# A hybrid attention and state-space step: chunk recurrence by pairs, fours and eights, the taps' own-input term in one operation, and a new placing of side steps

## The chip, the cores and the metric

The kernel runs on one core of one Trainium2 chip. The time is the device time of one execution in microseconds; the median of three runs before the change is 882.33 us. A core has five engines that this text names: TensorE (PE; its weight loads are PEld), VectorE (DVE), ScalarE (ACT), GpSimd (POOL) and SyncE (SP), which here issues all transfers (DMAs).

## What is computed

One layer of a streaming encoder, on 512 frames of one new stream and 16 further frames of each of 8 running streams (640 rows in all, 1024 channels), all in float32:

```python
h = rmsnorm(x, norm_g) @ w_in                     # 1024 -> 8 x 1024
q, k, v, ga, u, gs, gl = split(h)
o = diff_attn(rmsnorm(q), rmsnorm(k), v)          # 8 heads, two softmax maps, chunk-causal
ya = (rmsnorm(o) * silu(ga)) @ w_attn_proj
# diagonal complex state space, 64 groups x 64 states, 16 channels each
bu_t = B u_t ;  h_t = a * h_(t-1) + bu_t ;  y_t = Re(C h_t) + D u_t
ys = gelu(y);  ys = ys * sigmoid(ys @ w_glu + b_glu)
ys = (ys * silu(gs)) @ w_ssm_proj
x  = x + (sigmoid(g_a) * ya + sigmoid(g_s) * ys) @ w_out
# returned: x, the new k and v, the last state of each stream
```

The sample streams attend to a cache of 256 past keys and start from given states.

## The kernel before

**Products.** Every float32 product with a weight is three products of fp32r halves: an operand is split into a high part (ScalarE copies it, `whi`, `xh`) and the rest (VectorE subtracts, `wlo`, `xl`), and `mm3` (L306) adds hi x hi, hi x lo and lo x hi in PSUM. `gemm_a` (L401) computes 128 rows by 512 columns at a time for q, k, v and the last projection, `gemm_b` (L427) one block of 128 columns of the others for 2 x 320 rows. Weights come in pieces of 512 KB into `wraw`, two ahead, and are split by `pump` (L375). `ORDER` (L1581) is the list of these products with the columns of each; the main loop (L1490) goes through it.

**Side steps.** All else (norms, attention, the state space, the samples) is written as Python generators that yield a condition. The planner `Weave` (L38) keeps a model clock for each engine while the program is built. Between any two groups of three matmuls the main loop polls the generators, and whichever is due by the model puts its next piece into the program. TensorE runs in exactly this order; the other engines' instructions are ordered by a scheduler with a timeline model. `DELAY` (L1518, about 120 entries) adds microseconds to the due time of single steps, `GAPS` (L1553) a general gap in four stages. `lighter(bias)` (L63) picks VectorE or GpSimd for an elementwise piece: VectorE if its modelled queue ends before GpSimd's plus the bias. `W.hold()` moves the model's due time past the last transfer's landing. None of these is an instruction.

**The state space.** Time is cut into chunks of 8 frames: 64 chunks of the prompt, 2 for each sample stream. `ssm_setup` computes the powers of a, `ssm_f` and `ssm_in` the contribution of each chunk's inputs to the state at its end (`so`, stored as `s_d`). `ssm_tap` (L763) builds, in four parts q of 16 groups, `E` (powers times C, elementwise on VectorE or GpSimd, stored as `e_d`) and from it the taps: the direct effect of an input on the 8 outputs of its chunk. Its matmuls use plain float32 and a stationary operand of 32 columns, so that each writes 32 of the 128 PSUM partitions (index i) and 128 of 512 columns (index g). ScalarE copies the 128x512 result to `tp`; VectorE adds D u, the own-input term, to the first of the 8 taps, in four operations of 16 columns per q. `Es` has one buffer.

**The recurrence.** `states` (L1064) loads the 89 columns of chunk contributions as `R` (128 partitions x real/imaginary x 32 groups x 89): columns 0 to 15 are the samples' two chunks for 8 streams, 16 to 23 their start states, 24 to 88 the prompt. `cstep` takes a column range src to dst: two products with `a8` (a to the 8th, the step over one chunk), an addition, and an addition into R. It runs for the samples in 8 steps of 2 columns on GpSimd, and for the prompt 64 times, one column after the other, in pairs of steps that go to the engine that `lighter(ST_B)` names. Then `R` goes back to memory (`r_d`), for the output stage. The main loop has other waits on side steps: `kB` waits until the first half's 16 score steps are placed, `vB` until the first half's attention is stored; the samples' scores begin after the q's and `states`.

**Norms.** `norm_rows` (L815) and `subnorm` (L928) square on ScalarE, reduce on VectorE, and take the power -1/2 on GpSimd (`rs`, `osc`), then VectorE multiplies; TensorE then transposes the result (`kn`, `qn`, `o`).

Of the kernel before, what the change touches and what calls it, by code (L numbers as in the profile page):

```python
# [10 lines left out]
F32 = mybir.dt.float32  # L11
F32R = mybir.dt.float32r
AF = mybir.ActivationFunctionType
OP = mybir.AluOpType
# [8 lines left out]
RC = 89  # L23
# [170 lines left out]
CHAIN = object()  # L194
# [61 lines left out]
def trunk(nc, tc, a):  # L256
    es = ExitStack()
    enter = es.enter_context
    W = Weave(nc)
    PE, DV, AC, PL, SP = W.PE, W.DV, W.AC, W.PL, W.SP  # L260
# [17 lines left out]
    def mark(name):  # L278
        done.setdefault(name, []).append(W.t)
# [259 lines left out]
    a8 = pers.tile([128, 2, 2, 32], F32, name="a8")  # L539
# [223 lines left out]
    def ssm_tap(tpe):  # L763
        dT = tpe.tile([128, 4, 4], F32, name="dT")
        SP.dma_start(dT, a["dT"])
        dm = tpe.tile([128, 16], F32, name="dm")
        PL.tensor_tensor(dm, ident[:, 0:16], ident[:, 32:48], op=OP.add)
        PL.tensor_tensor(dm, dm, ident[:, 64:80], op=OP.add)
        PL.tensor_tensor(dm, dm, ident[:, 96:112], op=OP.add)
        PL.memset(bbs[:, 64], 0.0)  # L770


# [2 lines left out]
        tp = tpz[:, 7:]  # L775
        sh = [128, 4, 9, 16]
        for q in range(4):
            Es = tpe.tile([128, 4, 4, 144], F32, name="E", tag="E", bufs=1)
            for i in range(4):
# [5 lines left out]
                E = Es[:, i].rearrange("p g (j n) -> p g j n", n=16)  # L785
                Et = tpe.tile(sh, F32, name="Et", tag="Et", bufs=1)
                en = W.lighter()
# [3 lines left out]
                SP.dma_start(e_d[:, g4, :].rearrange("p g c -> p (g c)"), Es[:, i].rearrange("p g c -> p (g c)"))  # L791
                yield room("pv") if i == 3 else None
            pt = ps_pv()
            for i in range(4):
                for g in range(4):
                    gb = 16 * q + 4 * i + g
                    PE.matmul(pt[i * 32:i * 32 + 32, g * 128:g * 128 + 128],
                              bbs[:, gb:gb + 2, :].rearrange("p g n -> p (g n)"), Es[:, i, g, :128], start=True, stop=True)
            AC.activation(tp, pt.rearrange("p (g j n) -> p j g n", g=4, j=8), AF.Copy)
            for g in range(4):  # L800
                DV.scalar_tensor_tensor(tp[:, 0, g], dm, dT[:, q, g:g + 1], tp[:, 0, g], op0=OP.mult, op1=OP.add)
            SP.dma_start(tap_d[4 * q:4 * q + 4].rearrange("b n c -> (b n) c"), tpz.rearrange("p j g n -> p (j g n)"))
        mark("tap")

# [256 lines left out]

    def states(t3):  # L1064
        def cstep(E, dst, src, n):
            sh = [128, 2, 32, n]
            m1, m2 = (t3.tile(sh, F32, name="m12", tag=f"m{n}", bufs=2) for _ in range(2))
            E.tensor_tensor(m1, a8[:, 0, :, :, None].to_broadcast(sh), R[:, :, :, src:src + n], op=OP.mult)
            E.tensor_tensor(m2, a8[:, 1, :, :, None].to_broadcast(sh), R[:, ::-1, :, src:src + n], op=OP.mult)
            E.tensor_tensor(m1, m1, m2, op=OP.add)  # L1070
            E.tensor_tensor(R[:, :, :, dst:dst + n], R[:, :, :, dst:dst + n], m1, op=OP.add)

        R = t3.tile([128, 2, 32, RC], F32, name="R")
        SP.dma_start(R, s_d.rearrange("h p r g c -> (h p) r g c"))
        h0 = t3.tile([128, 2, 32, 8], F32, name="h0")
        SP.dma_start(h0, a["h0"])
        W.hold()
        yield
        AC.activation(R[:, :, :, 16:24], h0, AF.Copy)
        for d in (8, 0):  # L1080
            for i in range(0, 8, 2):
                cstep(PL, d + i, d + 8 + i, 2)
            yield CHAIN
        PL.tensor_copy(h0, R[:, :, :, 0:8])
        SP.dma_start(a["ss"], h0)
        for c in range(25, RC):
            if (c - 25) % ST_N == 0:
                yield CHAIN
                en = W.lighter(ST_B)
            cstep(en, c, c - 1, 1)  # L1090
        last = t3.tile([128, 2, 32], F32, name="last")
        PL.tensor_copy(last, R[:, :, :, RC - 1])
        SP.dma_start(a["sp"], last)
        SP.dma_start(r_d.rearrange("h p r g c -> (h p) r g c"), R)
        W.hold()
        mark("states")
# [393 lines left out]
    for n, opn, cols in ORDER:  # L1490
# [14 lines left out]
            gemm_a(op, evacs[n], *((lambda t: after("x", t + 1), FIRST) if n == "vA" else (None, GROUPS) if n == "o0" else ()))  # L1505
        else:
            gemm_b(op, evacs[n], cols, *((3, lambda i: after("og" if i else "og0")) if n == "ap" else ()))
        mark(n)
        if n == X_LAST:
            mark("xdone")  # L1510
        W.poll()
    pclose("ops", "yp")
# [3 lines left out]
COUNTERS = "hf", "t", "h4", "b", "b2", "first", "q", "x", "ct", "i", "gp", "m"  # L1516

DELAY = {  # L1518
# [30 lines left out]
}  # L1549
ACC = 0.6  # L1550
HALVES = slice(0, 64), slice(64, 128)
LATENCY = {"PE": 0.28, "AC": 0.2, "DV": 0.06, "PL": 0.3, "SP": 0.1}
GAPS = 1.3, 0.8, 0.4, 0.2  # L1553
SB = 3
WT = 2
ST_AT = 0
ST_N = 2
ST_B = 0.0
LANES = 3
SPB = 1  # L1560
# [3 lines left out]
TOB = 1  # L1564
KH = 4
VH = 6
X_LAST = "xs"
WRAW = 2
AHEAD = 5
FT = 2  # L1570
BIAS = 2.0
WARM = 10
GROUPS = ((0,), (1,), (2,), (3, 4))
FIRST = ((0,), (1,), (2,), (3,), (4,))
# [2 lines left out]
def cols(*names):  # L1577
    return [(n[0], n[1], range(*n[2:])) for n in names]


ORDER = [("vA", "x", None), ("u", "x", range(8)), ("kA", "x", None), ("ga", "x", range(8)), ("qA", "x", None),  # L1581
         ("gs", "x", range(0, 7)), ("kB", "x", None), ("qB", "x", None), ("vB", "x", None), ("gs", "x", range(7, 8)), ("xa", "x", range(0, 8)), ("xs", "x", range(0, 8)),
         ("ap", "og", range(8)), ("gl", "y", range(8)), ("sp", "y2", range(8)),
         ("o0", "m", None), ("o1", "m", None)]


OUTS = {"y": (TOK, 1024), "nk": (TOK, 1024), "nv": (TOK, 1024), "sp": (128, 2, 32), "ss": (128, 2, 32, 8)}

# [84 lines left out]
```

## Time and profile before

| | before |
|---|---|
| median of 3 runs | 882.33 us (880.16 to 882.72) |
| the profiled execution | 887.47 us, span 885.7 us |
| TensorE busy | 847.1 us, 5692 matmuls |
| VectorE busy | 558.9 us |
| ScalarE busy | 373.0 us |
| GpSimd busy | 253.0 us |
| mean granted TensorE clock | 0.987 of full speed |
| moved by DMA | 167.4 MB, 189 GB/s |

The span goes from the first to the last instruction; 1.8 us of the profiled execution lie around it. Busy times of different engines overlap. Matmuls are pipelined and one record's duration is longer than the distance to the next, so the idle time of TensorE is read from the gaps and the waits, not from single durations. Two full levels of the clock occur, 1.2 and 2.4 GHz; a share between is a mean over a stretch.

### The profile page before, as it was taken

Reading aid. Unit: us, or ns where it says so; the run is one execution under the profiler, and the core shown is the slowest. Engines: PE = TensorE matmul, PEld = TensorE weight load, DVE = VectorE, ACT = ScalarE, POOL = GpSimd, SP = SyncE. Lnnn points to the kernel's source line nnn. Section 1 sums busy time; section 2 is a strip of 40 time slices with the busy share of each in tenths; the row PEclk is TensorE's granted clock in tenths of the full one; section 3 lists DMA queues with packets and bytes.
Section 4 is the critical chain, followed back from the end, with each engine's and each line's share of the span. In section 5 each row is a group of like instructions: output and inputs, shape, how many; then the busy total and the mean of one; then the engine's idle time right before and its main releaser. Section 6 shows DMA issues by size and latency. Waiting matters only on the chain.

```text
span 885.7 us, 15567 instructions
## 1 busy us (share of the span) xinstructions
PE 847.1 (96%) x5692; PEld 776.9 (88%) x5692; DVE 558.9 (63%) x1267; ACT 373.0 (42%) x784; POOL 253.0 (29%) x426
## 2 busy tenths in 40 slices
PE   8999899889899989989999999999999999999998
PEld 6898889789789888767899887789999999999886
DVE  6688449886857788575667764224577755555321
ACT  6432227444236455233555544433565643422110
POOL 3734435323022996879810120000000000000000
PEclk8999899999899999999999999999999999999999
DMA  7365747564818531352585499958989763355231
GB/s 301 97 196 165 224 149 231 163 222 161 263 53 276 161 114 52 102 164 65 170 312 182 155 294 370 353 183 245 290 261 299 226 237 117 105 150 181 95 120 60
DMA packets 96445, 167.42 MB, mean 189 GB/s; under 512 B 16752, under 2 KB 54256, under 8 KB 96112
## 3 DMA queue, kind: packets, MB, share of 16 engines
q1 hardware_dynamic: 96368, 166.42, 59.1%
q8 instruction: 45, 0.74, 0.3%
q14 instruction: 32, 0.26, 0.1%
HBM read 118.45 MB, written 43.75 MB: 183 GB/s over the span
## 4 chain that ended last, share of the span: by engine, by line
PE 62%; POOL 12%; DMA 10%; DVE 10%; issue 3%; ACT 2%; SPq 1%; POOLq 0%; DVEq 0%; ACTq 0%
PE ps_mm L243 50%; POOL m L243 6%; PE ps_s L243 6%; DMA wraw<-in_wb_dram 4%; PE ps_pv L243 3%; PE ps_tp L243 3%; POOL R L243 3%; DVE wlo L243 2%; POOL rs L243 1%; ACT whi L243 1%; DMA svt<-in_cv_dram 1%; DMA H<-r_d 1%; DMA Ef<-e_d 1%; DMA u_d<-ue 1%; DVE kTl L243 1%
## 5 line engine op out<-in xcount | busy, mean ns | idle before, releaser
L243 PE MATMUL ps_mm<-xh,whi 128*128 128x320 f32 x640 | 205.5, 321 | 5.5 <-DVE ue L243 5.5
L243 PE MATMUL ps_mm<-xh,wlo 128*128 128x320 f32 x640 | 199.4, 312 | 0.0
L243 PE MATMUL ps_mm<-xl,whi 128*128 128x320 f32 x640 | 199.3, 311 | 0.0
L243 DVE TENSOR_TENSOR wlo<-wraw,whi 128x1024 fp32r<-128x1024 f32 x96 | 119.8, 1249 | 77.7 <-ACT whi L243 77.1
L243 ACT ACTIVATE whi<-wraw 128x1024 fp32r<-128x1024 f32 x96 | 101.6, 1059 | 109.7 <-PE ps_mm L243 79.6
L243 PEld LDWEIGHTS ps_mm<-xh,whi 128*128 128x128 f32 x640 | 121.9, 190 | 10.8 <-DVE ue L243 6.0
L243 PEld LDWEIGHTS ps_mm<-xl,whi 128*128 128x128 f32 x640 | 121.9, 190 | 0.8
L243 PEld LDWEIGHTS ps_mm<-xh,wlo 128*128 128x128 f32 x640 | 121.6, 190 | 0.0
L243 PE MATMUL ps_mm<-whi,xh 128*128 128x512 f32 x240 | 99.0, 412 | 0.9 <-ACT xh L243 0.9
L243 PE MATMUL ps_mm<-wlo,xh 128*128 128x512 f32 x240 | 95.6, 398 | 0.2 <-DVE wlo L243 0.2
L243 PE MATMUL ps_mm<-whi,xl 128*128 128x512 f32 x240 | 95.6, 398 | 0.0
L243 POOL TENSOR_TENSOR m<-a,R 128x64 f32<-128x64 f32 (+1 forms) x132 | 52.1, 418 | 15.4 <-DMA R<-s_d 8.2
L243 PEld LDWEIGHTS ps_mm<-whi,xl 128*128 128x128 f32 x240 | 46.1, 192 | 10.6 <-DVE xl L243 0.6
L243 PEld LDWEIGHTS ps_mm<-wlo,xh 128*128 128x128 f32 x240 | 46.3, 193 | 9.5 <-DVE wlo L243 1.4
L243 PEld LDWEIGHTS ps_mm<-whi,xh 128*128 128x128 f32 x240 | 46.3, 193 | 9.4 <-ACT xh L243 1.2
L243 POOL TENSOR_TENSOR rs<-ss,mhalf 128x8 f32<-128x8 f32 x20 | 32.9, 1645 | 40.8 <-DVE ss L243 40.6
L243 PE MATMUL ps_mm<-ogh,whi 128*128 128x320 f32 x128 | 41.0, 320 | 0.0
L243 PE MATMUL ps_mm<-yl,whi 128*128 128x320 f32 x128 | 39.6, 309 | 0.0
L243 PE MATMUL ps_mm<-yh,wlo 128*128 128x320 f32 x128 | 39.6, 309 | 0.0
L243 PE MATMUL ps_mm<-y2h,whi 128*128 128x320 f32 x128 | 39.6, 309 | 0.0
L243 PE MATMUL ps_mm<-y2h,wlo 128*128 128x320 f32 x128 | 39.6, 309 | 0.0
L243 PE MATMUL ps_mm<-y2l,whi 128*128 128x320 f32 x128 | 39.6, 309 | 0.0
(291 smaller groups left out, 1887.4 us busy)
## 6 DMA issues: line engine op xcount, KB each, us to landing
wraw<-in_wb_dram SPq DMA_DIRECT2D x64, 512.0 KB, 4.5
wraw<-in_wa_dram SPq DMA_DIRECT2D x32, 512.0 KB, 4.1
u<-u_d SPq DMA_DIRECT2D x16, 640.0 KB, 5.4
skt<-in_ckt_dram SPq DMA_DIRECT2D x16, 512.0 KB, 5.4
svt<-in_cv_dram SPq DMA_DIRECT2D x16, 512.0 KB, 8.0
u_d<-ue SPq DMA_DIRECT2D x16, 320.0 KB, 5.1
gate_xa<-gate SPq DMA_DIRECT2D x16, 320.0 KB, 4.1
e_d<-E SPq DMA_DIRECT2D x16, 288.0 KB, 3.4
```

The lines of the kernel that those rows point to most:

```text
L243: r = fn(out, *args, **kw)
```

## The change

Four things change.

1. `ssm_tap`: the loops over i and g of the tap matmuls change places, so that i runs inside. `dd`, the diagonal times D for all four q, is computed once by one VectorE product of 256 columns. Per q one VectorE addition of 64 columns reads the first tap from PSUM, adds `dd` and writes `tp`; ScalarE copies only the other seven taps. The planner holds for the transfer of `dT`.
2. `states`: `a16`, `a32`, `a64` are squared from `a8` by 18 small VectorE operations. The samples take one step of 8 columns for each of the two chunks. The prompt's chunks are combined in pairs (32, four pieces of 8), fours (16, two pieces), eights (8, one), then seven single steps over eights, then down again (7, 15 and 31 columns). Each piece is a `cstep` of up to 8 columns with a stride, on the engine that `lighter` names. The products' tile `m` has one tag with two buffers, which `h0` and the new `h1` share.
3. `DELAY` has new entries, `GAPS[2]` goes from 0.4 to 0.0 and `BIAS` from 2.0 to 1.36.
4. `ORDER`: the last column of `gs` comes after four columns of `xa`, and the columns of `xa` and `xs` are interleaved. `mark` and the end of the x operand's use follow the new list.

```diff
     def ssm_tap(tpe):
         dT = tpe.tile([128, 4, 4], F32, name="dT")
         SP.dma_start(dT, a["dT"])
+        W.hold()
...
+        dd = tpe.tile([128, 4, 4, 16], F32, name="dd")
+        sh = [128, 4, 4, 16]
+        DV.tensor_tensor(dd, dm[:, None, None, :].to_broadcast(sh), dT[:, :, :, None].to_broadcast(sh), op=OP.mult)
...
-            for i in range(4):
-                for g in range(4):
+            for g in range(4):
+                for i in range(4):
                     gb = 16 * q + 4 * i + g
                     PE.matmul(pt[i * 32:i * 32 + 32, g * 128:g * 128 + 128],
                               bbs[:, gb:gb + 2, :].rearrange("p g n -> p (g n)"), Es[:, i, g, :128], start=True, stop=True)
-            AC.activation(tp, pt.rearrange("p (g j n) -> p j g n", g=4, j=8), AF.Copy)
-            for g in range(4):
-                DV.scalar_tensor_tensor(tp[:, 0, g], dm, dT[:, q, g:g + 1], tp[:, 0, g], op0=OP.mult, op1=OP.add)
+            pj = pt.rearrange("p (g j n) -> p j g n", g=4, j=8)
+            DV.tensor_tensor(tp[:, 0], dd[:, q], pj[:, 0], op=OP.add)
+            AC.activation(tp[:, 1:], pj[:, 1:], AF.Copy)
...
     def states(t3):
-        def cstep(E, dst, src, n):
+        def cstep(E, A, dst, src, n, step=1):
             sh = [128, 2, 32, n]
-            m1, m2 = (t3.tile(sh, F32, name="m12", tag=f"m{n}", bufs=2) for _ in range(2))
...
+            cols = [slice(x, x + step * (n - 1) + 1, step) for x in (dst, src)]
+            m1, m2 = (t3.tile([128, 2, 32, ST_W], F32, name="m", tag="m", bufs=2)[:, :, :, :n] for _ in range(2))
+            E.tensor_tensor(m1, A[:, 0, :, :, None].to_broadcast(sh), R[:, :, :, cols[1]], op=OP.mult)
+            E.tensor_tensor(m2, A[:, 1, :, :, None].to_broadcast(sh), R[:, ::-1, :, cols[1]], op=OP.mult)
             E.tensor_tensor(m1, m1, m2, op=OP.add)
-            E.tensor_tensor(R[:, :, :, dst:dst + n], R[:, :, :, dst:dst + n], m1, op=OP.add)
+            E.tensor_tensor(R[:, :, :, cols[0]], R[:, :, :, cols[0]], m1, op=OP.add)
...
+        A = [a8] + [t3.tile([128, 2, 2, 32], F32, name=f"a{x}") for x in (16, 32, 64)]
...
         for d in (8, 0):
-            for i in range(0, 8, 2):
-                cstep(PL, d + i, d + 8 + i, 2)
-            yield CHAIN
-        PL.tensor_copy(h0, R[:, :, :, 0:8])
-        SP.dma_start(a["ss"], h0)
-        for c in range(25, RC):
-            if (c - 25) % ST_N == 0:
+            for i in range(0, 8, ST_W):
+                cstep(PL, a8, d + i, d + 8 + i, ST_W)
                 yield CHAIN
-                en = W.lighter(ST_B)
-            cstep(en, c, c - 1, 1)
+        h1 = t3.tile([128, 2, 32, 8], F32, name="h1", tag="m", bufs=2)
+        PL.tensor_copy(h1, R[:, :, :, 0:8])
+        SP.dma_start(a["ss"], h1)
+        up = [(A[x], 24 + (2 << x), 24 + (1 << x), 32 >> x, 2 << x) for x in range(3)]
+        row = [(A[3], 32 + 8 * k, 24 + 8 * k, 1, 1) for k in range(1, 8)]
+        down = [(A[x], 24 + (3 << x), 24 + (2 << x), (32 >> x) - 1, 2 << x) for x in (2, 1, 0)]
+        for Ax, dst, src, n, step in up + row + down:
+            for k in range(0, n, ST_W):
+                yield CHAIN
+                cstep(W.lighter(ST_B), Ax, dst + k * step, src + k * step, min(ST_W, n - k), step)
...
-GAPS = 1.3, 0.8, 0.4, 0.2
+GAPS = 1.3, 0.8, 0.0, 0.2
...
-BIAS = 2.0
+BIAS = 1.36
...
-         ("gs", "x", range(0, 7)), ("kB", "x", None), ("qB", "x", None), ("vB", "x", None), ("gs", "x", range(7, 8)), ("xa", "x", range(0, 8)), ("xs", "x", range(0, 8)),
-         ("ap", "og", range(8)), ("gl", "y", range(8)), ("sp", "y2", range(8)),
+         ("gs", "x", range(0, 7)), ("kB", "x", None), ("qB", "x", None), ("vB", "x", None), ("xa", "x", range(0, 4)),
+         ("gs", "x", range(7, 8)), ("xa", "x", range(4, 5)), ("xs", "x", range(0, 3)), ("xa", "x", range(5, 8)),
+         ("xs", "x", range(3, 8)), ("ap", "og", range(0, 8)), ("gl", "y", range(0, 8)), ("sp", "y2", range(0, 8)),
```

## Rows read from the trace of the kernel before

**Rows 1.** The page, busy times: us, share of the span, instructions.
```profile
PE 847.1 (96%) x5692; PEld 776.9 (88%) x5692; DVE 558.9 (63%) x1267; ACT 373.0 (42%) x784; POOL 253.0 (29%) x426
```
**Rows 2.** Sums by stretch: length, busy us (instructions) of each engine, granted clock, DMA.
```profile
140.00:240.00 100.00, 89.60 (x666) 86.65 (x665) 83.48 (x166) 45.34 (x107) 28.52 (x26) 0.95 0.66 209
220.00:240.00 20.00, 15.83 (x114) 14.90 (x113) 16.62 (x36) 7.50 (x20) 0.16 (x1) 0.86 0.77 253
300.00:440.00 140.00, 127.50 (x702) 108.86 (x701) 100.43 (x247) 60.58 (x131) 118.53 (x248) 1.00 0.37 108
712.00:880.00 168.00, 168.00 (x1024) 158.95 (x1023) 79.20 (x135) 45.97 (x73) 0.00 (x0) 1.00 0.42 136
```
**Rows 3.** TensorE's waits, whole span: releaser, us in total, times, longest.
```profile
PE ps_s L243 <- DVE tap L243: 4.2, 1, 4.2
PE ps_s L243 <- DVE so L243: 4.0, 3, 2.1
PE ps_tp L243 <- DVE kn L243: 2.8, 2, 2.2
```
**Rows 4.** Timeline of TensorE: start, us, operation, records; a tap group, one of scores.
```profile
229.12 2.46 PE L243 MATMUL ps_pv<-E,bbs 128*32 128x128 f32 x32
...
496.23 1.12 PE L243 MATMUL ps_s<-skt,qbd 128*32 128x272 f32 x16
```
**Rows 5.** Timeline after the first tap group, all engines; idle before and releaser in brackets.
```profile
163.54 3.10 DVE L243 SCALAR_TENSOR_TENSOR tap<-dm,dT,tap 128x16 f32<-128x16 f32 x3 [1.00 <-ACT tap L243]
...
165.21 1.40 POOL L243 TENSOR_TENSOR E<-E,Et 128x576 f32<-128x576 f32 x1
...
166.56 0.24 DVE L243 SCALAR_TENSOR_TENSOR so<-ps_s,sgn,so 128x32 f32<-128x32 f32 x1
...
166.95 0.31 PE L243 MATMUL ps_s<-u,Wh 128*128 128x160 f32 x1 [2.14 <-DVE so L243]
```
**Rows 6.** Timeline after the third tap group, VectorE and TensorE.
```profile
234.24 0.76 DVE L243 TENSOR_TENSOR E<-P,cc 128x576 f32<-128x576 f32 x1 [1.35 <-DMA wraw<-in_wb_dram]
...
235.75 0.47 PE L243 MATMUL ps_s<-u,Wh 128*128 128x160 f32 x1 [4.17 <-DVE tap L243]
```
**Rows 7.** Groups of VectorE by form: busy us, mean ns, idle before and releaser.
```profile
L243 DVE TENSOR_TENSOR o<-o,ps_pv 128x128 f32<-128x128 f32 x32 | 9.0, 281 | 1.5 <-ACT o L243 1.5
...
L243 DVE SCALAR_TENSOR_TENSOR tap<-dm,dT,tap 128x16 f32<-128x16 f32 x16 | 6.3, 447 | 1.0 <-ACT tap L243 1.0
```
**Rows 8.** Single tiles (`tap`, `F`, `P`): ns least/median/most, first and last start, forms.
```profile
L243 DVE SCALAR_TENSOR_TENSOR tap<-dm,dT,tap x16: 225/230/1430, 163.5 to 268.9; 128x16 f32<-128x16 f32 x16
...
L243 DVE TENSOR_TENSOR F<-F,Ft x9: 678/687/1646, 84.0 to 199.5; 128x512 f32<-128x512 f32 x9
...
L243 POOL TENSOR_TENSOR F<-F,Ft x7: 1265/1297/2157, 130.6 to 211.4; 128x512 f32<-128x512 f32 x7
...
L243 POOL TENSOR_TENSOR Ft<-P,bbi x7: 1100/1112/1544, 84.8 to 200.3; 128x512 f32<-128x512 f32 x7
```
**Rows 9.** Sum over the recurrence, tile `m` alone: length, DVE busy, POOL busy, clock, DMA.
```profile
284.00:441.00 157.00, 5.86 (x24) 109.47 (x264) 1.00 0.41 120
```
**Rows 10.** Timeline at the start of the recurrence, GpSimd and ScalarE.
```profile
284.57 0.67 POOL L243 TENSOR_TENSOR m<-a,R 128x64 f32<-128x64 f32 x2 [8.19 <-DMA R<-s_d]
...
287.57 0.67 ACT L243 ACTIVATE R<-h 128x512 f32<-128x512 f32 x1
```
**Rows 11.** Timeline of a key's norm within the recurrence, three engines.
```profile
394.86 1.64 POOL L243 TENSOR_TENSOR rs<-ss,mhalf 128x8 f32<-128x8 f32 x1
...
396.53 0.69 DVE L243 TENSOR_TENSOR kn<-ps_mm,rs 128x512 f32<-128x512 f32 x1 [1.84 <-POOL rs L243]
...
398.65 0.52 PE L243 MATMUL ps_tp<-ident,kn 128*128 128x128 f32 x3 [2.15 <-DVE kn L243]
```
**Rows 12.** Groups of GpSimd by form from 300 to 440: the powers of the norms.
```profile
L243 POOL TENSOR_TENSOR rs<-ss,mhalf 128x8 f32<-128x8 f32 x10 | 16.4, 1642 | 0.0
L243 POOL TENSOR_TENSOR osc<-oss,mhalf 128x4 f32<-128x4 f32 x4 | 4.9, 1235 | 0.0
```

More of the change, by code (lines that the diff above doesn't have):

```diff
@@ L1064, in states @@
     def states(t3):
-        def cstep(E, dst, src, n):
+        def cstep(E, A, dst, src, n, step=1):
             sh = [128, 2, 32, n]
-            m1, m2 = (t3.tile(sh, F32, name="m12", tag=f"m{n}", bufs=2) for _ in range(2))
-            E.tensor_tensor(m1, a8[:, 0, :, :, None].to_broadcast(sh), R[:, :, :, src:src + n], op=OP.mult)
-            E.tensor_tensor(m2, a8[:, 1, :, :, None].to_broadcast(sh), R[:, ::-1, :, src:src + n], op=OP.mult)
+            cols = [slice(x, x + step * (n - 1) + 1, step) for x in (dst, src)]
+            m1, m2 = (t3.tile([128, 2, 32, ST_W], F32, name="m", tag="m", bufs=2)[:, :, :, :n] for _ in range(2))
+            E.tensor_tensor(m1, A[:, 0, :, :, None].to_broadcast(sh), R[:, :, :, cols[1]], op=OP.mult)
+            E.tensor_tensor(m2, A[:, 1, :, :, None].to_broadcast(sh), R[:, ::-1, :, cols[1]], op=OP.mult)
             E.tensor_tensor(m1, m1, m2, op=OP.add)
-            E.tensor_tensor(R[:, :, :, dst:dst + n], R[:, :, :, dst:dst + n], m1, op=OP.add)
+            E.tensor_tensor(R[:, :, :, cols[0]], R[:, :, :, cols[0]], m1, op=OP.add)
         R = t3.tile([128, 2, 32, RC], F32, name="R")
         SP.dma_start(R, s_d.rearrange("h p r g c -> (h p) r g c"))
-        h0 = t3.tile([128, 2, 32, 8], F32, name="h0")
+        h0 = t3.tile([128, 2, 32, 8], F32, name="h0", tag="m", bufs=2)
         SP.dma_start(h0, a["h0"])
+        A = [a8] + [t3.tile([128, 2, 2, 32], F32, name=f"a{x}") for x in (16, 32, 64)]
+        sq = t3.tile([128, 32], F32, name="sq")
+        for x, y in zip(A, A[1:]):
+            re, im = x[:, 0, 0], x[:, 1, 1]
+            DV.tensor_tensor(sq, im, im, op=OP.mult)
+            DV.tensor_tensor(y[:, 0, 0], re, re, op=OP.mult)
+            DV.tensor_tensor(y[:, 0, 0], y[:, 0, 0], sq, op=OP.subtract)
+            DV.tensor_scalar(y[:, 0, 1], y[:, 0, 0], 1.0, None, op0=OP.mult)
+            DV.scalar_tensor_tensor(y[:, 1, 0], re, -2.0, im, op0=OP.mult, op1=OP.mult)
+            DV.scalar_tensor_tensor(y[:, 1, 1], re, 2.0, im, op0=OP.mult, op1=OP.mult)
+            yield CHAIN
         W.hold()
@@ L1080, in states @@
         for d in (8, 0):
-            for i in range(0, 8, 2):
-                cstep(PL, d + i, d + 8 + i, 2)
-            yield CHAIN
-        PL.tensor_copy(h0, R[:, :, :, 0:8])
-        SP.dma_start(a["ss"], h0)
-        for c in range(25, RC):
-            if (c - 25) % ST_N == 0:
-                yield CHAIN
-                en = W.lighter(ST_B)
-            cstep(en, c, c - 1, 1)
+            for i in range(0, 8, ST_W):
+                cstep(PL, a8, d + i, d + 8 + i, ST_W)
+                yield CHAIN
+        h1 = t3.tile([128, 2, 32, 8], F32, name="h1", tag="m", bufs=2)
[6 more added lines that the diff above has]
+            for k in range(0, n, ST_W):
+                yield CHAIN
+                cstep(W.lighter(ST_B), Ax, dst + k * step, src + k * step, min(ST_W, n - k), step)
         last = t3.tile([128, 2, 32], F32, name="last")
@@ L1507, in trunk @@
             gemm_b(op, evacs[n], cols, *((3, lambda i: after("og" if i else "og0")) if n == "ap" else ()))
-        mark(n)
-        if n == X_LAST:
+        if n in ("u", "ap"):
+            mark(n)
+        if (n, cols) == X_LAST:
             mark("xdone")
@@ L1556 @@
 ST_AT = 0
-ST_N = 2
+ST_W = 8
 ST_B = 0.0
@@ L1566 @@
 VH = 6
-X_LAST = "xs"
 WRAW = 2
@@ L1578, in cols @@
     return [(n[0], n[1], range(*n[2:])) for n in names]
-ORDER = [("vA", "x", None), ("u", "x", range(8)), ("kA", "x", None), ("ga", "x", range(8)), ("qA", "x", None),
-         ("gs", "x", range(0, 7)), ("kB", "x", None), ("qB", "x", None), ("vB", "x", None), ("gs", "x", range(7, 8)), ("xa", "x", range(0, 8)), ("xs", "x", range(0, 8)),
-         ("ap", "og", range(8)), ("gl", "y", range(8)), ("sp", "y2", range(8)),
+ORDER = [("vA", "x", None), ("u", "x", range(0, 8)), ("kA", "x", None), ("ga", "x", range(0, 8)), ("qA", "x", None),
+         ("gs", "x", range(0, 7)), ("kB", "x", None), ("qB", "x", None), ("vB", "x", None), ("xa", "x", range(0, 4)),
+         ("gs", "x", range(7, 8)), ("xa", "x", range(4, 5)), ("xs", "x", range(0, 3)), ("xa", "x", range(5, 8)),
+         ("xs", "x", range(3, 8)), ("ap", "og", range(0, 8)), ("gl", "y", range(0, 8)), ("sp", "y2", range(0, 8)),
          ("o0", "m", None), ("o1", "m", None)]
+X_LAST = [(n, cols) for n, operand, cols in ORDER if operand == "x"][-1]
 OUTS = {"y": (TOK, 1024), "nk": (TOK, 1024), "nv": (TOK, 1024), "sp": (128, 2, 32), "ss": (128, 2, 32, 8)}
```

59 rows, old and new, of the table DELAY are left out of this document.

## The prediction, made before the change was built

> **What bounds the kernel now.** I began with the page's busy times: TensorE is busy 847.1 us of a span of 885.7 [rows 1]. So the time is TensorE's work plus its idle time (38.6 us) plus what a lowered clock costs. The change leaves the matrix products as they are, so I looked for places where TensorE stands still or works badly, and asked which of them the change touches. The sums by stage show where that is: 10.4 us of idle time in 140 to 240 and 12.5 us in 300 to 440, while from 712 on TensorE never stops [rows 2]. An edit can pay in the first two stretches only. Third, TensorE's waits by releaser: VectorE's `tap` operations once for 4.2 us, its `so` evacuations three times for 4.0 us, its `kn` 2.8 us [rows 3]. They are single waits, not a steady shortage. In 300 to 440 GpSimd is the busiest engine after TensorE, 118.5 of 140 us [rows 2], nearly all of it the recurrence of `states`.
>
> **Part 1, the taps' matmuls.** This is the one edit that shortens TensorE's own work. Today the 16 products of one q are issued with i outside: four in a row go to the same 32 output partitions. Such a group shows as 32 records (each product is two) that take 2.46 us, and there are four groups [rows 4]. The new order lets i run inside, so neighbours go to four different strips of 32 partitions. The sample scores have that pattern already: 16 records of 272 columns, strips in turn, take 1.12 us [rows 4]. That is 16 x 272 = 4352 columns; a tap group has 32 x 128 = 4096, so I estimate 1.12 x 4096 / 4352 = 1.05 us, and allow 1.1. A group saves 1.36 us. Bounds: 0 (no overlap) and 1.41. The group near 229 is followed at once by a wait that VectorE ends [rows 4, 6], so there the gain only lengthens the wait; I count three: **-4.1 us**.
>
> **Part 2, the taps' own-input term.** Today ScalarE copies the whole 128x512 result out, and only then VectorE runs four small operations per q. 16 of them cost 6.3 us, 447 ns on average [rows 7], though 225 is the least [rows 8]. In the first group VectorE sat idle 1.00 us for the copy, then three took 3.10 us, and `so`, which TensorE needed, came at 166.56; TensorE had waited 2.14 us [rows 5]. After, one addition reads PSUM directly and is no longer behind ScalarE's copy. It has 64 columns; the nearest rows are the 128-column addition from PSUM at 281 ns and the small operation at 225 [rows 7, 8], so 0.28 us. At the first group that frees VectorE about 1.0 + 3.1 - 0.3 = 3.8 us earlier, more than the 2.14 us: **-2.1 us** (bounds 0 and -2.1). The same queue holds ScalarE's `so` copies behind a slightly shorter tap copy, which costs nothing.
>
> The 4.17 us wait at 235.75 is another matter. The profile names `tap`, but VectorE had before that stood 1.35 us at an `E` whose release was a transfer, then worked through `E` and the taps [rows 6]. With the operations in the same order the taps leave only 0.45 us there: **-0.45**, bounds 0 and -7.0. The far end is the whole wait plus the clock: the stretch 220 to 240 was granted 0.86 [rows 2], that is part of it at 1.2 instead of 2.4 GHz after that idle time, and 0.14 x 20 = 2.8 us of work is lost by it.
>
> New is `dd`, one product of 256 columns on VectorE before 90 us, between 0.28 (128 columns) and 0.69 us (512) [rows 7, 8], once. It also waits for the `dT` transfer, and behind it on VectorE's queue stand the first `E`, which need their own later transfer (`cc`) in any case. Cost 0, at most 0.7 if VectorE is the last to finish there. Holding the planner's clock until `dT` has landed adds no instruction.
>
> **Part 3, the recurrence.** It now runs 64 chunk steps one after the other, four operations each, 64 columns wide, and 8 sample steps of 128 columns: together 109.5 us of GpSimd and 5.9 of VectorE, from 284 to 441 [rows 9]. After: seven steps up (4 + 2 + 1), seven in a row, seven down (1 + 2 + 4), and two for the samples. 16 of the 23 are up to 8 chunks wide: 512 columns. No row shows that form of this step; the nearest are the 512-column operations for `F`: a product at 1.11 and the addition at 1.30 on GpSimd, 0.69 on VectorE [rows 8]. A wide step is then 2 x 1.11 + 2 x 1.30 = 4.8 us on GpSimd, or 2.8 on VectorE. A narrow one stays at 109.5 us over 66 steps, 1.7 us with the wider ones counted in, so at most that. All on GpSimd: 16 x 4.8 + 7 x 1.7 = 89 us, 20 less than today. Before, 24 of 288 instructions went to VectorE [rows 9]; the rule that chooses is the same, so I leave one step in ten there. Strided columns could make the wide form dearer; the old narrow form reads with a stride too. Bounds for the stage: 60 us (half on VectorE) and 110.
>
> What does it bring TensorE? Nothing waits for `states` but the samples, and TensorE has other columns to compute then; an earlier end alone is worth **0**. Two waits are added. `m`, `h0` and `h1` now share two buffers. The first wide step waits for ScalarE's copy of `h0`, done at 288.2, where today the chunk steps start at 284.6 [rows 10]: 3.6 us of GpSimd's time. Later a step waits until `h1` is stored. Queued behind on GpSimd are the powers of the norms; nobody else. The 18 small operations for the squared coefficients (near 0.23 us each by [rows 8], some 4 us) fall on VectorE while `R` is in flight: 0, at most +1.
>
> **Part 4, delays and order.** The table of delays, `GAPS`, `BIAS` and the order of the `gs`, `xa` and `xs` columns change where side steps fall among matmuls; columns cost the same anywhere, and the weights' transfers keep their number. No row prices this. It can take away stalls or make them: all idle time of both stretches, 22.9 us, is the one bound, and half as much more the other. For the middle I let idle time shrink as the load on the feeding engine does: VectorE in 140 to 240 loses about 16 x 0.447 - 4 x 0.28 = 6 of 83.5 us, 7% of 10.4 us; GpSimd in 300 to 440 loses some 18 of 118.5, 15% of 12.5 us: **-2.6 us**.
>
> **Sum.** -4.1 - 2.1 - 0.45 - 2.6 = -9.3 us. The profiled execution took 887.5 us (span 885.7 and 1.8 around it), so it would become 878.2. The median of the runs is 882.3, 5.1 lower; I carry the gain over in microseconds: **873.0 us**, 1.1% faster.
>
> **Rivals.** (a) *Slower: wide steps in the way of the norms.* GpSimd also computes the powers for `kn`, `qn` and `o`. At 394.86 such a power came between two operations of a chunk step; VectorE's `kn` waited 1.84 us for it and TensorE 2.15 us for `kn` [rows 11]. A step once queued will hold GpSimd 4.8 us where two chunk steps held it about 3.4. Also VectorE and GpSimd hinder each other: a `tap` operation beside GpSimd's `E` took up to 1.43 us against 0.23 and ended with it [rows 5, 8]. With operations of 1.1 to 1.3 us VectorE may wait up to 1.2 us where an operation of the present step lasts 109.5 / 264 = 0.41 [rows 9]. Price: 14 powers in the stretch [rows 12], each later by (4.8 - 3.4) / 2 = 0.7, and two VectorE operations behind each by 0.4 more: 14 x 1.5 = 21 us if all reaches TensorE. With the 6.7 us of parts 1 and 2 that is 897; with two thirds of it, 890. It decides for slower once more than 9.3 of the 21 us arrive. Against it: 12.5 us of idle time is all that the stretch shows today with GpSimd at 85%, and that share falls.
>
> The Trainium skill, page SBUF — State Buffer, section "SBUF: two separate sides", speaks against this change: it says that a VectorE operation with two SBUF inputs and a GpSimd operation take a shared pair of ports exclusively, for the whole instruction, and the other blocks fully. The 1.43 us row agrees with it; by this rule the case just priced would be the outcome, about 890.
>
> (b) *Much faster.* The wait at 235 with its clock goes, the fourth tap group counts too, and half the idle time of 300 to 440 goes: 4.1 + 1.4 + 2.1 + 7.0 + 6.3 = 21 us, 861.
>
> (c) *Nothing to measure.* The tap groups don't overlap, or TensorE runs sooner into the same evacuations; only some 2 us stay: 880 to 881.
>
> **Chances.** Forecast 0.57 (866 to 879.7), (b) 0.15, (c) 0.14, (a) 0.14. About 0.3% (2.6 us) is what a measurement of this kernel can tell from no change. Faster 0.72, same 0.14, slower 0.14. The range 862 to 886 leaves out the lower half of (b) and the larger part of (a).
>
> **What would show it.** Right: tap groups near 1.1 us; four `tap` additions of 64 columns near 0.3 us; no TensorE wait on `tap`; operations on `m` near 90 us on GpSimd in far fewer instructions, ended before 430. Wrong: groups still over 2 us; a TensorE wait on `kn` above today's 2.8 us; VectorE's two-input operations over 1 us beside GpSimd; new stalls outside both stretches.

## The result: 1.2% slower

The median of the kernel after is 892.41 us (891.24 to 893.47, four runs), that of the kernel before beside it 881.25 us; the ratio is 1.0120, 95% interval 1.0095 to 1.0146. The forecast was 873.0 us. The rows after that answer to [rows 1 and 2], the page's busy times and the sums by stretch (length, then busy us and instructions of TensorE, its weight loads, VectorE, ScalarE and GpSimd, granted clock, DMA share, GB/s):

```profile
PE 847.8 (95%) x5692; PEld 775.6 (87%) x5692; DVE 583.4 (66%) x1259; ACT 372.9 (42%) x784; POOL 249.5 (28%) x245
...
140.00:240.00 100.00, 92.49 (x685) 87.69 (x684) 86.22 (x160) 44.44 (x107) 35.39 (x31) 0.93 0.71 221
300.00:440.00 140.00, 123.97 (x664) 107.09 (x663) 114.07 (x215) 57.16 (x120) 107.66 (x92) 0.97 0.45 140
712.00:880.00 168.00, 166.40 (x1033) 157.57 (x1032) 80.27 (x137) 47.26 (x76) 0.00 (x0) 1.00 0.41 134
```

In 300 to 440 TensorE gets through 664 instructions instead of 702. GpSimd is less busy there than before (107.7 us against 118.5), as forecast; VectorE has fewer instructions (215 against 247) and is busy 13.6 us longer. That contradiction is the trail: VectorE's operations have become longer. The waits of TensorE, as [rows 3]:

```profile
PE ps_pv L243 <- DVE o L243: 7.6, 4, 4.3
PE ps_s L243 <- DVE so L243: 6.5, 5, 4.1
```

The wait on `o` for these products was, in the kernel before:

```profile
PE ps_pv L243 <- DVE o L243: 0.6, 2, 0.3
```

The wait on `tap` is gone. In its place stands one of 4.1 us on `so` at 223, and the one on `o` has grown from 0.6 to 7.6 us; it lies in the stage of the recurrence. The tap groups, as [rows 4], the additions to the first tap, and the recurrence's tile `m` on GpSimd (ns least, median, most; first and last start; forms; then idle time of its engine):

```profile
159.05 1.08 PE L243 MATMUL ps_pv<-E,bbs 128*32 128x128 f32 x32
...
228.94 1.94 PE L243 MATMUL ps_pv<-E,bbs 128*32 128x128 f32 x32
...
L243 DVE TENSOR_TENSOR tap<-dd,ps_pv x4: 209/214/223, 161.2 to 261.5; 128x64 f32<-128x64 f32 x4
...
L243 POOL TENSOR_TENSOR m<-a,R x40: 353/1155/2316, 281.9 to 407.7; 128x512 f32<-128x512 f32 x26, 128x64 f32<-128x64 f32 x10, 128x448 f32<-128x448 f32 x4
L243 POOL TENSOR_TENSOR R<-R,m x20: 427/1332/2397, 286.4 to 411.7; 128x512 f32<-128x512 f32 x13, 128x64 f32<-128x64 f32 x5, 128x448 f32<-128x448 f32 x2
...
  DMA out_ss_dram<-h: 1.5, 1
```

And the place where the longest new wait arises (timeline, three engines; idle before and releaser in brackets):

```profile
319.52 1.29 POOL L243 TENSOR_TENSOR m<-m 128x512 f32<-128x512 f32 x1
319.58 1.25 DVE L243 TENSOR_TENSOR osc<-osc,orz 128x4 f32<-128x4 f32 x1 [0.53 <-POOL osc L243]
...
320.89 1.85 POOL L243 TENSOR_TENSOR R<-R,m 128x512 f32<-128x512 f32 x1
...
321.95 1.87 DVE L243 TENSOR_TENSOR wlo<-wraw,whi 128x1024 fp32r<-128x1024 f32 x1
...
322.68 3.60 POOL L243 TENSOR_TENSOR m<-a,R 128x512 f32<-128x512 f32 x2
...
324.95 0.39 PE L243 MATMUL ps_pv<-vt,wth 128*128 128x256 f32 x1 [4.30 <-DVE o L243]
```

A VectorE operation of 4 columns lasts 1.25 us, from the start to the end of a GpSimd addition of 512 columns. Then `wlo`, 1.2 us at its shortest, takes 1.87, and GpSimd's next two products 3.60 where another pair takes 2.26. TensorE stands 4.3 us for the `o` at the end of VectorE's queue.

### The profile page after: what moved, and what is told of

It reads as the page before. It is cut to its first block, busy times and chain, and to the rows that moved or that the text cites. A ratio compares the mean times of both kernels' runs of the same rounds, so it can differ in the third digit from the quotient of the medians.

```text
span 890.5 us, 15373 instructions
## 1 busy us (share of the span) xinstructions
PE 847.8 (95%) x5692; PEld 775.6 (87%) x5692; DVE 583.4 (66%) x1259; ACT 372.9 (42%) x784; POOL 249.5 (28%) x245
## 4 chain that ended last, share of the span: by engine, by line
PE 61%; DVE 17%; DMA 9%; POOL 5%; issue 4%; ACT 3%; SPq 1%; ACTq 0%; DVEq 0%; POOLq 0%
PE ps_mm L243 49%; PE ps_s L243 6%; PE ps_tp L243 3%; DVE wlo L243 3%; PE ps_pv L243 3%; DMA wraw<-in_wb_dram 2%; POOL m L243 2%; DVE sb L243 1%; DMA cc<-in_cC_dram 1%; POOL rs L243 1%; ACT whi L243 1%; DMA H<-r_d 1%; DVE oss L243 1%; DVE kn L243 1%; DMA svt<-in_cv_dram 1%
## 5 line engine op out<-in xcount | busy, mean ns | idle before, releaser
L243 DVE TENSOR_TENSOR wlo<-wraw,whi 128x1024 fp32r<-128x1024 f32 x96 | 123.3, 1286 | 72.9 <-ACT whi L243 69.3
L243 POOL TENSOR_TENSOR m<-a,R 128x512 f32<-128x512 f32 (+2 forms) x40 | 45.6, 1160 | 13.7 <-PE ps_s L243 11.7
L243 PE MATMUL ps_mm<-yh,whi 128*128 128x320 f32 x128 | 39.7, 310 | 0.5 <-ACT yh L243 0.5
```

Source lines behind the costliest of these rows:

```text
L243: r = fn(out, *args, **kw)
```

## The experiments

Ratios are to the kernel before, run on the same chip beside each kernel. "Same plan" means that the planner is charged as in the kernel after, so that TensorE's instructions stay in the same order; the order on the other engines is settled later, by durations, and can come out differently.

### One part at a time

First the same kernel again, then each part alone or left out. The diffs are those of the change, limited to `ssm_tap` (taps alone), to `states` (recurrence alone), to all but `states` (old recurrence), and to `DELAY`, `GAPS`, `BIAS` and `ORDER` (placing alone).

> The kernel before once more, for a second profile of it and for the spread of the comparison. Every theory: ratio 1.000 within 0.002. The first profile of it was 5 us longer than its own median; if that was the one execution and not the profiling, this profile should be near 881 to 883 us.

> The kernel before with the edits of the taps alone (loops exchanged, dd, one addition per q); old recurrence, old delays, old order. Theory R (the taps gain, the recurrence loses): four tap groups near 1.1 us, TensorE waits on tap gone, 4.1 to 4.7 us gained, so 876 to 877.5 against 881.2. Theory Q (the gain only lengthens the next wait): 880 to 881.5.

> The kernel before with the new recurrence alone; old taps, old delays, old order. Theory R: the pieces of 512 columns cost TensorE about 10 us between 256 and 454, so 889 to 893. Theory P (what loses is the new placing, delays and order of columns): 879 to 882, as the predicted price of the recurrence for TensorE was nothing.

> The kernel after with the old recurrence: new taps, new delays, new order of columns, but 64 chunk steps one after the other. Theory R: the loss goes with the new recurrence, 874 to 879. Theory P: the loss stays, 887 to 892.

> The kernel before with the new delays, gaps, bias and order of columns alone; old taps, old recurrence. The prediction's term for this part: -2.6 us, so 879. From the kernel with the taps as well (880.6) and the taps' gain of 4.1: 884 to 885. If the delays were worth nothing without the recurrence that they go with: 885 to 895.

| taps | recurrence | placing | ratio, 95% interval |
|---|---|---|---|
| old | old | old | 1.0013 [0.9989, 1.0037] |
| new | old | old | 1.0038 [1.0009, 1.0067] |
| old | new | old | 1.0320 [1.0293, 1.0346] |
| old | old | new | 1.0047 [1.0027, 1.0067] |
| new | old | new | 0.9990 [0.9970, 1.0009] |
| new | new | new | 1.0120 [1.0095, 1.0146] |

The loss goes with the recurrence: without it the change is neutral, with it alone the kernel loses 29 us, three times what I had expected of it. The parts don't add up. Taps and placing each lose 3 to 4 us alone and nothing together; taps and placing together take some 18 us off the new recurrence (29 to 11), and no run has the new recurrence with only one of them. Neither of my two theories had foreseen that taps alone cost time.

The second profile of the kernel before took 879.45 us; the first took 887.47, 5 us above the median. TensorE from 84 to 100, first in the old profile, then in the new one:

```profile
84.00:92.00 8.00, 3.80 (x27) 0.94 0.31 94
92.00:100.00 8.00, 8.00 (x37) 0.64 0.84 218
```

```profile
84.00:92.00 8.00, 5.04 (x35) 1.00 0.39 118
92.00:100.00 8.00, 8.00 (x56) 1.00 0.94 241
```

In the first execution TensorE waited 4.2 us for `ue`, in the second 3.0, and after the first the clock was at the lower level for part of the next 8 us: 19 products fewer, at 0.147 us each 2.8 us. With the 1.2 us of wait that is 4.0 of the 8.0 us between the two profiles.

### Narrow operations, and GpSimd held in other ways

Three kernels with the same plan. In the first each operation of the recurrence is one column wide on the chip:

```diff
-            E.tensor_tensor(m1, A[:, 0, :, :, None].to_broadcast(sh), R[:, :, :, cols[1]], op=OP.mult)
+            go((m1, ...), f1, A[:, 0, :, :, None].to_broadcast(s1), R[:, :, :, r1[1]], OP.mult)   # f1 = m1[..., :1]
```

The second and third fill each formerly wide GpSimd operation up to its old length:

```diff
                 E.e.tensor_tensor(out, in0, in1, op=op)
+                    E.e.memset(hold, 0.0)                        # second kernel, twice; hold is m1 or m2
+                    E.e.tensor_copy(hold, R[:, :, :, cols[1]])   # third kernel, twice
```

> The kernel after, TensorE's instructions in the same order, but each operation of the recurrence is one column wide on the chip instead of up to eight (left out: up to seven of eight columns of every step, so the states of the prompt are not computed in full). Theories L and H (the wide operations cost the 10 us, by whichever way): VectorE's time above the least of each form in 280 to 440 falls from 34.6 us to some 10 to 12 as before the change, and the time to 879 to 884. Theory P (the number or the place of the steps costs it, not their width): 889 to 893.

> As the kernel with one column, but on GpSimd each operation that was 448 or 512 columns wide is filled up to its old length, some 1.4 us, by two memsets, which read nothing (left out: the same columns). GpSimd's queue is held as long as in the kernel after. Theory H (the norms' powers wait behind a step in GpSimd's queue): 889 to 894, as the kernel after. Theory L (VectorE and GpSimd keep each other from reading or writing memory, queue or not): VectorE's time above the least near 12 us and 880 to 885, as with one column; if memsets block VectorE as much as products do, 889 to 894 with VectorE's operations as long as in the kernel after, and then this run doesn't tell L from H.

> As the kernel with memsets, but GpSimd is held by copies of 512 columns (one input read, 0.64 us each, two per operation) instead of memsets (left out: up to seven of eight columns of every step). Theory L as the Trainium skill's page SBUF has it (reading is what locks the shared ports): VectorE's time above the least rises towards 34.6 us and the time to 885 to 892. If only operations with two inputs shut VectorE out: 872 to 876, as with memsets.

One column: 873.61 us, ratio 0.9916 [0.9893, 0.9939]. Memsets: 872.39, 0.9910 [0.9883, 0.9936]. So the wide operations cost 20 us of 892.4 (18.5 by the ratios), and that is not GpSimd's queue: with memsets it is held just as long (93.1 us on the tile `m` against 96.1), and the time is that of the narrow kernel. One reservation: the three steps on VectorE are narrower too, 3.3 us instead of 6.3. Another: both kernels are faster than any theory said, and faster than the complete kernel with the old recurrence and the same taps and placing (0.9990), though with memsets VectorE is not delayed less. Its time above the shortest of each form, summed from 280 to 440, is 10.4 us with the old recurrence, 11.8 with memsets and 34.5 in the kernel after. Where that further 0.8% comes from the runs don't show. Groups of VectorE from 300 to 400 (busy us, mean ns; idle before): three of the kernel before (second profile), then after, then with memsets:

```profile
L243 DVE TENSOR_TENSOR wlo<-wraw,whi 128x1024 fp32r<-128x1024 f32 x8 | 10.1, 1268 | 1.6 <-ACT whi L243 1.6
L243 DVE TENSOR_TENSOR kn<-kn,gk 128x512 f32<-128x512 f32 x5 | 3.8, 763 | 0.1
L243 DVE TENSOR_TENSOR oss<-oss,orz 128x4 f32<-128x4 f32 x6 | 1.4, 238 | 0.1
```

```profile
L243 DVE TENSOR_TENSOR wlo<-wraw,whi 128x1024 fp32r<-128x1024 f32 x8 | 13.9, 1743 | 0.0
L243 DVE TENSOR_TENSOR kn<-kn,gk 128x512 f32<-128x512 f32 x4 | 5.5, 1384 | 0.0
L243 DVE SCALAR_TENSOR_TENSOR sb<-s,c,sb 128x384 f32<-128x384 f32 x4 | 5.5, 1365 | 0.1
L243 DVE SCALAR_TENSOR_TENSOR gate<-gate,ps_mm 128x320 f32<-128x320 f32 x8 | 3.9, 482 | 0.1
L243 DVE TENSOR_TENSOR oss<-oss,orz 128x4 f32<-128x4 f32 x6 | 2.8, 465 | 0.1
```

```profile
L243 DVE TENSOR_TENSOR wlo<-wraw,whi 128x1024 fp32r<-128x1024 f32 x8 | 10.1, 1258 | 2.4 <-ACT whi L243 2.4
L243 DVE SCALAR_TENSOR_TENSOR gate<-gate,ps_mm 128x320 f32<-128x320 f32 x8 | 3.9, 483 | 1.3 <-ACT gate L243 1.3
L243 DVE TENSOR_TENSOR kn<-kn,gk 128x512 f32<-128x512 f32 x5 | 3.4, 682 | 0.0
L243 DVE SCALAR_TENSOR_TENSOR sb<-s,c,sb 128x384 f32<-128x384 f32 x4 | 2.6, 653 | 0.1
L243 DVE TENSOR_TENSOR oss<-oss,orz 128x4 f32<-128x4 f32 x6 | 1.1, 179 | 0.1
```

With memsets `kn`, `sb` and `oss` need half the time or less, `wlo` 0.5 us less, about as before the change; `gate`, which reads PSUM, is the same. TensorE between 256 and 456, after and with memsets: 99 instructions more in the same 200 us.

```profile
256.00:456.00 200.00, 181.17 (x1044) 159.36 (x1043) 163.88 (x376) 93.77 (x220) 128.96 (x111) 0.97 0.49 151
```

```profile
256.00:456.00 200.00, 192.24 (x1143) 171.03 (x1141) 150.06 (x409) 103.50 (x241) 126.73 (x232) 0.99 0.53 167
```

The kernel with copies took 965.22 us, but not for the reason it was made. GpSimd's order came out differently: powers of the norms precede steps of the recurrence, and GpSimd stands 54 us for the sums that they need from VectorE, VectorE itself 24 us for a step of the recurrence. That ends at 522 us, the first `qbd` of the samples stands behind it on GpSimd, and TensorE waits 77.1 us for it. The total says nothing on copies; the stage does. I took each VectorE operation that began during the recurrence, its time above the shortest of its form in the same run (its excess), and what GpSimd was doing at that moment (count, mean excess in ns, share of those over 200 ns). "Two inputs" are operations on two operands in SBUF; "others" are reciprocals, reductions and accumulator reads in SBUF:

| GpSimd is in | kernel | VectorE, two inputs | VectorE, others | VectorE, an operand in PSUM |
|---|---|---|---|---|
| product or sum, 64 columns | before, again | 38, 95 ns, 8% | 39, 16 ns, 0% | 53, 10 ns, 0% |
| product or sum, 512 columns | after | 31, 639 ns, 77% | 30, 13 ns, 0% | 50, 14 ns, 0% |
| copy, 512 columns | copies | 28, 473 ns, 79% | 27, 7 ns, 0% | 46, 13 ns, 0% |
| memset, 512 columns | memsets | 28, 9 ns, 0% | 26, 14 ns, 0% | 42, 33 ns, 2% |

So my alternative, that only GpSimd operations with two inputs block, is wrong: a copy does too. What the memset lacks is an input. Left out of the table are VectorE's small `tensor_scalar` operations, which have one input and are held in both kernels: 743 ns beside products (4 of them), 842 beside memsets (4). With them the operations in SBUF beside wide products are 65, 356 ns above their shortest on average: 23 us of VectorE's time in the stage.

The Trainium skill, page SBUF — State Buffer, section "SBUF: two separate sides", has this rule: VectorE with two SBUF inputs and GpSimd take the shared port pair from each other for a whole instruction, but "only against a GpSimd op that reads SBUF"; a VectorE operation in what the page calls a 2-port perf mode takes it too. The table agrees with the first part: two-input operations are held beside products and copies (639 and 473 ns) and not beside memsets (9 ns). The `tensor_scalar` operations would fit the second, but which mode they ran in no run shows.

### Shorter pieces

Two kernels change `ST_W` to 2 and to 4 and are planned anew; the third keeps the plan of the kernel after and issues each step as two of up to 4 columns:

```diff
+            for c0 in range(0, n, 4):
+                c = slice(c0, min(c0 + 4, n))
...
+                E.e.tensor_tensor(m1[:, :, :, c], b0, r1[:, :, :, c], op=OP.mult)
...
```

> The kernel after with pieces of 2 columns: the same tree, 71 steps, operations of 128 columns near 0.47 us on GpSimd instead of 1.3 us. Complete. Theory L or H: a VectorE operation or a power is held 0.5 us or 1.9 us instead of 1.3 or 5.4, so most of the 10 us come back: 881 to 886. Theory P: 889 to 893. GpSimd's total grows by some 10 to 20 us; if GpSimd's total decided, it would be above 893.

> The kernel after with pieces of 4 columns: operations of 256 columns near 0.75 us on GpSimd. Complete. Theory L or H: between the kernel with pieces of 2 and the kernel after, 884 to 890. Theory P: 889 to 893.

> The kernel after with the same planned order, but each step of up to 8 columns is issued as two of up to 4: operations of 256 columns, 0.7 to 0.8 us instead of 1.1 to 1.3. Complete. Theory L1 (what counts is how long one GpSimd operation shuts VectorE out): VectorE's time above the least in 280 to 440 near 20 us instead of 34.6, and about half of the loss returns, 880 to 886. Theory L2 (what counts is the total time in which GpSimd reads, which stays): 890 to 894.

All three missed: 931.65 us (1.0590 [1.0523, 1.0658]), 898.11 (1.0193 [1.0158, 1.0228]) and 897.66 (1.0195 [1.0159, 1.0231]), slower than the kernel after. The first two were planned anew with delays made for another plan: with pieces of 2 the recurrence ends at 467 instead of 412, and TensorE stands 10.3 us for `osm` later. VectorE's excess from 280 to 440 does fall with the width, from 34.5 us to 20.4 (pieces of 4) and 16.4 (pieces of 2), but GpSimd's time on the tile `m` grows from 96.1 us to 108.3 and 136.5, and the total with it. With pieces of 2 it lies where my expectation had put it if GpSimd's total decides; no run separates that total from the late end and the new plan. The third kernel is the clean one, and it shows two effects. The mean excess of VectorE's operations in SBUF beside a GpSimd operation falls from 356 to 241 ns, and TensorE is ahead of the kernel after until 419. Then (SyncE's queue, start and duration; its wait; TensorE):

```profile
417.81 0.33 SPq L243 DMA_DIRECT2D r_d<-R  x1
418.88 0.33 SPq L243 DMA_DIRECT2D wraw<-in_wa_dram  x1
...
SPq L243 <- POOL R L1087: 3.1, 1, 3.1
...
432.11 0.80 PE L243 MATMUL ps_mm<-whi,xh 128*128 128x512 f32 x1 [5.54 <-ACT whi L243]
```

GpSimd's work is longer in short pieces (104.8 us against 96.1), the recurrence ends 4 us later, SyncE stands 3.1 us for its store, and a transfer of weights is queued behind that store. It lands 12.1 us after its issue, where the one that follows the landed store in the kernel after takes 4.1. For those weights TensorE stands 5.5 us. So the end of the recurrence isn't free, and the prediction's "an earlier end alone is worth 0" holds only as long as it isn't later than the store's place in SyncE's queue.

### Where the taps' gain goes

The loops alone, in both directions, all else and the planned order kept:

```diff
-            for g in range(4):
-                for i in range(4):
+            for i in range(4):
+                for g in range(4):
```

> The kernel after with the two loops over the tap matmuls changed back, all else and the order of the instructions kept. Complete. It measures the term for the tap groups by itself: a group takes 2.46 us again instead of 1.08. Prediction's step (the gain reaches the end for three groups): 4 us slower than the kernel after, 896 to 897. Theory Q (the waits on so behind the groups swallow it): 891 to 893, as the kernel after.

> The kernel with the new placing alone (885.4) with the two loops over the tap matmuls exchanged, and nothing else. The gain of the groups by itself, 4 x 1.38 us = 5.5: 880 to 881.5. Theory Q (waits behind the groups swallow it, as in the kernel after with the loops changed back): 884 to 886.

Changed back in the kernel after: 891.31 us, 1.0123 [1.0092, 1.0154], as the kernel after, though the groups take 2.46 us again. Changed in the kernel with the placing alone: 884.05, 1.0027 [1.0003, 1.0051], against 1.0047: of the 5.5 us some 2 arrive, and as the intervals overlap, that can't be told from nothing. The second pair shows where it goes (TensorE by stretch; without, then with the new loops):

```profile
155.00:276.00 121.00, 113.38 (x774) 0.96 0.59 191
276.00:340.00 64.00, 57.98 (x396) 0.95 0.45 135
...
PE ps_pv L243 <- DVE o L243: 4.9, 1, 4.9
```

```profile
155.00:276.00 121.00, 113.49 (x816) 0.96 0.62 200
276.00:340.00 64.00, 55.12 (x352) 0.92 0.39 117
...
276.59 1.06 ACT L243 ACTIVATE whi<-wraw 128x1024 fp32r<-128x1024 f32 x1 [2.90 <-DMA wraw<-in_wb_dram]
...
PE ps_pv L243 <- DVE o L243: 8.9, 3, 4.1
```

The gain reaches TensorE in full by 276: 42 instructions more. Up to 340 it is given back: 44 fewer, and the wait on `o` grows from 4.9 to 8.9 us. TensorE now runs into weights that haven't landed (ScalarE idles 2.90 us for them, 0.54 at most from 262 to 300 without the new loops) and into the attention's chain over VectorE, neither of which the taps make faster.

Two further edits try to open what stands behind: `dT` loaded behind the third `bB`, near 64 us, so that VectorE doesn't stand for it; and the last F (b = 15) on GpSimd.

```diff
+                with tc.issue_after(bB.ins):
+                    SP.e.dma_start(dT, a["dT"])
...
+            if b == 15:
+                en = Meter(W, PL.e, en.n)
```

> The kernel after with one transfer moved: dT is loaded behind the third bB, near 64 us, instead of at 80 us; the planned order is kept. Complete. In the kernel after VectorE stood 1.3 us for dT before dd, with E and ue behind it, and TensorE then waited 3.6 us for ue and got the half clock. Theory D (dd's wait is passed on to TensorE): the wait on ue falls to 2 us or less, the clock stays at 1.00 from 88 to 100, and the time is 888 to 890. If another transfer or step is late in its place: 891 to 893.

> The same move of dT in the kernel with the old recurrence (880.6). Theory D: 877 to 878.5, faster than the kernel before. Otherwise 880 to 881.

> As the kernel with the old recurrence and dT early, and the three operations of the last F (b = 15) run on GpSimd instead of VectorE. In all kernels with the new placing TensorE waits 4.1 us for so near 223, and has the half clock for some 10 us behind it. Two of the three operations, 1.4 us, stand on VectorE ahead of those so. Theory S (that wait and its clock hold back the gain of the tap groups): the wait falls below 3 us, and the time to 871 to 875. If the last so is held by something else: 877 to 881.

The kernel after with `dT` early: 892.94, 1.0116 [1.0088, 1.0145]. With the old recurrence: 881.16, 0.9989 [0.9969, 1.0009]; with F moved as well: 881.78, 0.9989 [0.9969, 1.0009]. None differs from its kernel. VectorE's idle time before `dd` is gone (1.34 us in the kernel after, where `dT` lands at 84.9 and `dd` starts at 85.0) and TensorE's wait for `ue` falls from 3.6 to 2.8 us, but the medians don't show it. F on GpSimd shortens the wait for `so` at 223 from 4.1 to 3.9 us only: theory S as I stated it, two F operations ahead of `so`, is wrong. What holds that `so` I haven't shown: in the kernel after VectorE works without a gap from 219.25 to the end of the wait at 223.5, on a `wlo` (1.22 us), two `Wl` (0.68 each), F (0.68), a `gate` and the `so` operations. The best complete kernels, 0.9989 to 0.9990, can't be told from the kernel before.

## Why the prediction was wrong, step by step

**Bound and places.** Right in the main. Against the second profile of the kernel before, TensorE's idle time grows by 11.7 us (31.0 to 42.7), and 6.7 of them lie in 300 to 440 (9.4 to 16.0); 140 to 240 has 1.1 less. But 5.6 lie outside both stretches, where no edit was to matter: 2.4 before 140, 1.6 from 240 to 300 and 1.6 from 712 on.

**Part 1.** The group's price was right: 1.08 us against an estimate of 1.1. The step "I count three: -4.1" failed. Changing the loops alone moved the end by nothing in one kernel and by some 2 us, not clear of noise, in another; the gain is there until 276 and is then swallowed. The prediction had discounted only the group with a wait right behind it and not asked what bounds the stretch that follows.

**Part 2.** The addition takes 0.21 us (estimate 0.28) and the wait on `tap` is gone. The -2.1 us didn't arrive in the one kernel that tests them alone: with the taps alone TensorE waits at that point 4.1 us for `so`, since VectorE now does `wlo` (2.19 us) and an `E` (1.81) ahead of it, both 1 us above their shortest. Taking operations away had also changed VectorE's order, and the prediction had assumed the same order. In the kernel after TensorE doesn't stand at that point at all (busy for all 21 us from 155 to 176), but with the placing alone it hardly does either (20.86 of 21), so the gain isn't the taps'. `dd` at 0: VectorE stood 1.3 us for its transfer, twice the bound of 0.7, and removing that showed nothing in the medians.

**Part 3.** This is the miss. A wide step was put at 4.8 us on GpSimd and cost 6.0 (2 x 1.423 + 1.467 + 1.704, the means of these forms in the whole run; the shortest of each add up to 4.7); the total of 96.1 us against an estimate of 89 is a small error. The failing step is the answer to "What does it bring TensorE?", which was 0 for the recurrence: 20 us lie between the kernel after and the one with memsets in place of the wide operations, about as much as between forecast and result (19.4). What happened instead is that wide products and sums delay VectorE's two-input operations by 0.64 us on average, 20 us in the stage (23 with the `tensor_scalar` operations), and TensorE waits for VectorE. That the kernel with memsets lands on the forecast (872.4 against 873.0) is luck: the gains that make up the forecast are not there, since taps and placing with the old recurrence give 0.9990. Of the two added waits the one for the store of `h1` shows, as 1.5 us of GpSimd's time.

**Part 4.** -2.6 us was a guess by loads, and the runs show no such gain: placing alone is 0.5% slower, with the taps it makes up for what they lose, and together with them it takes 18 us off the recurrence. As I read it, a table of delays fits only the kernel that it was made for; no run tries other delays.

**Rivals.** (a) was priced at 890 and the result is 892.4, and its place and sign are right. Of its two mechanisms the queue (0.7 us for each power) is refuted by the memsets; the exclusion between VectorE and GpSimd is what happened, but it meets VectorE's two-input operations wherever they fall, not two behind each power, so that the price fits so well is luck too. Its threshold of 9.3 us counts the 2.6 of part 4, which its own 897 leaves out; by that sum it is 6.7. It got 0.14 on the ground that the stage showed little idle time. That argument was wrong: it looked at TensorE's waits under operations of 0.41 us and took them for those under 1.3 us.

**Base.** Carrying the gain over in microseconds did no harm; the first profile was a long execution, and one wait and the clock behind it make half of its distance to the second.

## What to carry to other kernels

Fewer, wider elementwise operations on GpSimd are no gain by themselves: beside a busy VectorE each wide one that reads SBUF delays VectorE's next two-input operation there by up to its own length. Narrower pieces shortened that delay here but held GpSimd longer and ended later, and brought nothing back. Price such a change on VectorE's queue as well as on GpSimd's total, and test it with memsets of the same length. A term that shortens TensorE's own work is worth something only if the next stretch isn't bound by a transfer or another engine's chain: ask where TensorE arrives earlier, and what isn't there yet.

## What the runs showed of the chip that I had not expected

- What delays VectorE's two-input operations is GpSimd's reading: copies of one input delay them by 473 ns on average, memsets of the same width by 9; VectorE operations with an operand in PSUM are 10 to 33 ns above their shortest whatever GpSimd does.
- TensorE's clock after a single wait differs from execution to execution. After a wait of 3.6 us for `ue` the stretch 92 to 100 was granted 0.79 in the kernel after and 1.00 in the one with the loops changed back; after 3.0 us it was 1.00 in the kernel before, and after 2.8 us 0.83 in the kernel after with `dT` early. Behind the 4.1 us wait for `so`, 224 to 236 ran at 0.50 in the kernel after: a tap group there takes 1.94 us instead of 1.08.
- The same program's profiled executions differed by 8 us (887.47 and 879.45), about half of it from that one place (1.2 us of wait and 2.8 of clock).
